# Block sums of Strassen-type weights: formed on VectorE, or added into SBUF by accumulating transfers

## Chip, cores and metric

The kernel runs on 1 core of one Trainium2 chip. The metric is device time in microseconds (us), the median of several runs. 1964.19 us is the median of 3 runs of the kernel before, which lie between 1963.92 and 1965.04 us.

## What is computed

The reference is a two-layer transformer on 512 tokens of width 1024. Each layer has a feed-forward network (FFN), a mixer, and a second FFN; there are four FFNs in all. The change is in the FFNs.

```python
def swiglu(h, w_in, w_out):
    a, b = jnp.split(h @ w_in, 2, axis=-1)
    return (jax.nn.silu(a) * b) @ w_out

for layer in range(DEPTH):
    g = norm_g[layer]
    x = x + 0.5 * swiglu(rmsnorm(x, g[0]), ffn_w_in[layer, 0], ffn_w_out[layer, 0])
    h = rmsnorm(x, g[1])
    ...
    x = x + 0.5 * swiglu(rmsnorm(x, g[2]), ffn_w_in[layer, 1], ffn_w_out[layer, 1])
```

`w_in` is 1024 x 5632, `w_out` 2816 x 1024, all float32.

## The kernel before

**Precision.** Every matrix is split into a high part (float32r, a rounded copy made on ScalarE, ACT) and a low part (the difference, made on VectorE, DVE). One product of two matrices is then three matmuls: high by high, high by low, low by high.

**Seven products.** `h @ w_in` is done with a scheme that needs seven products of half-size blocks in place of eight. The 22 tiles of each half of `w_in` go in 11 pairs. Each pair p has four weight blocks of 128 x 1024 floats (512 KB): a11, a21, a12 and a22. Its products take these left sides: p1 a11, p2 a12, p4 a22, and the sums p5 a21 + a22, p6 a21 + a22 - a11, p3 a12 - (a21 + a22 - a11), p7 a11 - a21. `Products.side` (lines 131 to 151) makes each sum with one VectorE instruction over 128 x 1024: L142, L145, L148, L150. `Products.make` (L153) then makes the split: `whi` on ScalarE (L159) and `wlo` on VectorE (L160), into a pool `wsp` with three slots of each. The right sides (sums of halves of x) are made once per FFN by `combined` (L215), tile by tile, into `th` and `tl`.

**Order of the work.** PE follows the program's order exactly. `round_` (L402) goes through a list of products; ahead of each it asks for the splits of the next three. One product is 24 matmuls (L332). `ORDER` (L105) is p1, p5, p2, p6, p3, p7, and p4 comes one pair later, behind the next pair's p1. In each FFN the pairs go in three rounds (0 to 4, 5 to 8, 9 and 10); behind each round stands a part of the product with `w_out` ("down", lines 383 to 397), which needs the results of the pairs so far. On the other engines a scheduler sets the order when the program is built.

**Loads.** All blocks come from DRAM on SP's queue (`fetch`, L121). `wraw` has two buffers, each with a pair's a11 and a21; a22 has two buffers and a12 one. A load waits till the split that last read its buffer is done.

**Norm.** The row scale is summed from `ss` (L255 on POOL), by four small matmuls (`rstd_cols`, L280, asked for at pair 0's p6), Ln and Exp on ScalarE (L267, L268), four small DVE steps (the last writes `Rc`, L272) and four transposes on PE (`rstd_rows`, L294, asked for at pair 0's p3).

**ScalarE's tables.** Ln, Exp and Silu need a function table. `lnexp` (L175) loads one that holds both Ln and Exp ahead of a stage that wants them; where a function's table isn't loaded, the build puts a load (ACT_TABLE_LOAD) ahead of the instruction.

Of the kernel before, what the change touches and what calls it, by code (L numbers as in the profile page):

```python
# [8 lines left out]
F32 = mybir.dt.float32  # L9
# [3 lines left out]
OP = mybir.AluOpType  # L13
# [28 lines left out]
class Filler:  # L42
# [5 lines left out]
    def add(self, name, gen):  # L48
        self.q.append((name, gen))
# [49 lines left out]
class Products:  # L99
# [2 lines left out]

    ORDER = ("p1", "p5", "p2", "p6", "p3", "p7", "p4")  # L105

    def __init__(self, b, src):
        self.b, self.src, self.parts, self.blocks = b, src, {}, {}
# [1 line left out]
    def place(self, p, early):  # L110
# [7 lines left out]
        else:  # L118
            w["a12"] = b.wx.tile([128, 1024], F32, name="a12", bufs=1)

    def fetch(self, p, n):  # L121
        c = ("a11", "a21", "a12", "a22").index(n) * 1024
        self.b.nc.sync.dma_start(self.blocks[p][n], self.src[p, :, c:c + 1024])

    def load(self, p, early):
        if p < NP and ("a11" if early else "a12") not in self.blocks.get(p, ()):
            self.place(p, early)
            for n in ("a11", "a21", "a22") if early else ("a12",):
                self.fetch(p, n)

    def side(self, p, q):

        w, v = self.blocks[p], self.b.nc.vector
        if q == "p1":
            return w["a11"]
        if q == "p2":
            return w["a12"]
        if q == "p4":
            return w["a22"]
        if q == "p5":  # L140
            w["s"] = self.b.wx.tile([128, 1024], F32, name="ws", bufs=1)
            v.tensor_add(w["s"], w["a21"], w["a22"])  # L142
            return w["s"]
        if q == "p6":
            v.tensor_sub(w["s"], w["s"], w["a11"])  # L145
            return w["s"]
        if q == "p3":
            v.tensor_sub(w["a12"], w["a12"], w["s"])  # L148
            return w["a12"]
        v.tensor_sub(w["a21"], w["a11"], w["a21"])  # L150
        return w["a21"]

    def make(self, p, q):  # L153
        if (p, q) in self.parts:
            return
        b = self.b
        x = self.side(p, q)
        o = b.wtile(1024)
        b.nc.scalar.activation(o[0], x, AF.Copy)  # L159
        b.nc.vector.tensor_sub(o[1], x, o[0].bitcast(F32))  # L160
        self.parts[p, q] = o


class Builder:
# [50 lines left out]
    def combined(self, i, gcol):  # L215

        nc, v = self.nc, self.nc.vector
        j, x = i // 2, self.X[:, i].rearrange("p (h t) -> p h t", h=2)

        def parts(n, m, src):  # L220
            h, l = self.TH[j][:, n:n + m], self.TL[j][:, n:n + m]
            nc.scalar.activation(h, src, AF.Copy)  # L222
            v.tensor_sub(l, src, h.bitcast(F32))  # L223

        if i % 2 == 0:

            e = self.E = self.xp.tile([128, 3, HT], F32, name="te")
            nc.scalar.activation(e[:, 0:3:2], x, AF.Copy, scale=gcol)
            v.tensor_sub(e[:, 1], e[:, 2], e[:, 0])
            parts(B11, 2, e[:, 0:2])  # L230
        else:

            e, o = self.E, self.xp.tile([128, 5, HT], F32, name="to")
            nc.scalar.activation(o[:, 0:2], x, AF.Copy, scale=gcol)
            parts(B21, 2, o[:, 0:2])
            v.tensor_sub(o[:, 2], o[:, 1], e[:, 1])
            v.tensor_sub(o[:, 3], o[:, 0], o[:, 2])
            v.tensor_sub(o[:, 4], o[:, 1], e[:, 2])
            parts(T2, 3, o[:, 2:5])

# [71 lines left out]
    def ffn(self, n, after, first=None):  # L312
# [5 lines left out]
        nc = self.nc  # L318
# [15 lines left out]
        def copy(name, bank, bufs):  # L334
            t = self.ft.tile([128, 2, HT], F32, name=name, bufs=bufs)
            nc.scalar.activation(t, bank.rearrange("p (f t) -> p f t", f=2), AF.Copy)
            return t

        def run(p, q, R):

            v = nc.vector
            three = lambda b: b.rearrange("p (f t) -> p f t", f=2)
            if q == "p1":
                d = st[p] = {"a": self.bank("ps")}
                product(p, q, d["a"], B11, True)
                d["c1"] = copy("c1", d["a"], 1)
                return
            d = st[p]
            if q == "p5":
                d["b"] = self.bank("pt")  # L350
                product(p, q, d["b"], T1, True)
                d["c5"] = copy("c5", d["b"], 1)
            elif q == "p2":
                c = self.bank("s")
                product(p, q, c, B21, True)
                d["t"] = self.ft.tile([128, 2, 2, HT], F32, name="ta", bufs=2)
                v.tensor_add(d["t"][:, :, 0], d["c1"], three(c))
            elif q == "p6":
                product(p, q, d["a"], T2, False)
                d["c2"] = copy("c2", d["a"], 1)  # L360
            elif q == "p3":
                product(p, q, d["b"], B22, False)
                v.tensor_add(d["t"][:, :, 1], d["c2"], three(d["b"]))
                t = d["t"].rearrange("p f h t -> p f (h t)")
                v.tensor_mul(t, t, R()[:, None, :].to_broadcast([128, 2, S]))
                self.table = "silu"
                nc.scalar.activation(t, t, AF.Silu)
            elif q == "p7":
                product(p, q, d["a"], T3, False)
                v.tensor_add(d["c5"], d["c5"], three(d["a"]))  # L370
            else:
                product(p, q, d["a"], T4, False)
                t = d["t"]
                v.tensor_mul(t[:, :, 1], t[:, :, 1], d["c5"])
                v.tensor_mul(t[:, :, 0], t[:, :, 0], three(d["a"]))
                h = [self.hp.tile([128, 2, S], F32R, name=x) for x in ("hh", "hl")]
                t = t.rearrange("p f h t -> p f (h t)")
                nc.scalar.activation(h[0], t, AF.Copy)
                v.tensor_sub(h[1], t, h[0].bitcast(F32))  # L379
                H[p] = h  # L380
                del st[p]
# [11 lines left out]

        def down_end(d, bank, R):
            t = self.ft.tile([128, S], F32, name="dn", bufs=1)
            nc.vector.scalar_tensor_tensor(t, bank, 0.5, R, op0=OP.mult, op1=OP.mult)  # L396
            nc.vector.tensor_add(self.X[:, d], self.X[:, d], t)

        tags = ("s", "s", "s", "pt", "o")
# [1 line left out]
        R = lambda: Rt[0]  # L401
# [19 lines left out]
        for g, (a, b) in enumerate(GROUPS):  # L421
            last = b == NP
            seq = []
            for p in range(a + 1 if g else a, min(b + 1, NP)):
                ps = [(p, q) for q in Products.ORDER[:6]]
                if p:
                    ps.insert(1, (p - 1, "p4"))
                seq += ps
            round_(a, seq + [(NP - 1, "p4")] * last)
            banks = {}  # L430

            def begin(d):
                w = down_w(g, d)
                w.split(0)
                banks[d] = w, self.bank(tags[d % 5])

            def sums(d, pairs):
                down_mm(g, d, *banks[d], pairs)

            def end(d):  # L440
                down_end(d, banks.pop(d)[1], R())
                if last:
                    after(d)

            begin(0)
            begin(1)
            if last:
                self.next_in()
                self.lnexp()
                sums(0, range(a, b - 1))  # L450
                run(NP - 1, "p4", R)
                sums(1, range(a, b - 1))
                for d in range(2):
                    sums(d, [b - 1])
                    end(d)
                begin(2)
            for d in range(2 if last else 0, KT):
                if d + 1 < KT and d + 1 not in banks:
                    begin(d + 1)
                sums(d, range(a, b))  # L460
                if d == KT - 2:
                    W.load(b + 1, True)
                end(d)
# [691 lines left out]
    def build(self):  # L1155
        from contextlib import ExitStack
        with ExitStack() as ctx:
            nc, tc = self.nc, self.tc
# [61 lines left out]
            first = None  # L1220
# [4 lines left out]
            if kind(0) == "ffn":  # L1225
                self.wx = tc.alloc_tile_pool(name="wx", bufs=1)
                first = Products(self, self.i["ffn_in"][int(st[0][3])])
                first.place(0, True)
                first.place(0, False)
                for i, n in ((0, 0), (1, "a11"), (2, 0), (3, "a21"), (4, 0), (5, "a22"), (6, 0), (7, "a12")):  # L1230
                    xdma(i)
                    if n:
                        first.fetch(0, n)
            else:
                for i in range(KT):
                    xdma(i)
# [116 lines left out]
```

## Time and profile before

| | |
|---|---|
| median of 3 runs | 1964.19 us |
| the profiled execution | 1967.51 us, its span 1965.6 us |
| PE busy | 1872.4 us, 95% |
| DVE busy | 1481.5 us, 75% |
| ACT busy | 908.5 us, 46% |
| POOL busy | 226.8 us, 12% |
| DMA | 198.16 MB, mean 101 GB/s |

Times are read from one profiled execution. "L332" is line 332 of the kernel. PE is TensorE's matmuls, PEld its weight loads, DVE VectorE, ACT ScalarE, POOL GpSimd, SP the engine that issues most transfers ("SPq" is an issue). An arrow `<-` behind an idle time names what ended it.

### The profile page before, as it was taken

What the parts mean: (1) busy time and instruction counts of PE and PEld (TensorE: products, weight loads), DVE (VectorE), ACT (ScalarE), POOL (GpSimd) and SP (SyncE); (2) the same over time, 40 slices, a digit from 0 to 9 for tenths busy, and PEclk for the clock granted to TensorE, in tenths of its full rate; (3) what the DMA queues carried; (4) which work ended last, traced back from release to release, by engine and by line L of the source; (5) the groups of instructions that cost most, each with busy time, mean ns of one, the idle gap of its engine ahead of it and who ended that gap; (6) DMA issues with size and microseconds to landing.
All of it is one profiled execution on the core that took longest, in us unless ns stands there. A gap on an engine that the chain in (4) does not pass through costs nothing.

```text
span 1965.6 us, 30669 instructions
## 1 busy us (share of the span) xinstructions
PE 1872.4 (95%) x12448; PEld 1682.0 (86%) x12448; DVE 1481.5 (75%) x1929; ACT 908.5 (46%) x1275; POOL 226.8 (12%) x218
## 2 busy tenths in 40 slices
PE   4999999999999899999979999999999989999997
PEld 3999989887877898999879899897776779989896
DVE  7977958657466895876889688675898688869684
ACT  5543525434354452443555345254537555435343
POOL 2000000200162000000010000002258320000001
PEclk9999999999899899999989999999999989999998
DMA  4333241313332224232313323224256132323412
GB/s 154 97 108 107 85 126 52 120 65 105 106 102 76 91 92 129 98 101 90 112 64 108 119 92 113 86 76 143 74 158 174 38 115 97 105 93 103 129 47 83
DMA packets 60509, 198.16 MB, mean 101 GB/s; under 512 B 7880, under 2 KB 8056, under 8 KB 57296
## 3 DMA queue, kind: packets, MB, share of 16 engines
q1 hardware_dynamic: 57712, 191.65, 30.8%
q10 hardware_dynamic: 2304, 4.20, 0.9%
q8 instruction: 97, 1.59, 0.3%
q0 software_dynamic: 352, 0.36, 0.1%
q14 instruction: 44, 0.36, 0.1%
HBM read 178.03 MB, written 2.15 MB: 92 GB/s over the span
## 4 chain that ended last, share of the span: by engine, by line
PE 82%; DVE 12%; ACT 2%; issue 2%; DMA 1%; SPq 0%; POOL 0%; DVEq 0%; ACTq 0%; POOLq 0%
PE ps L332 25%; PE pt L332 13%; PE s L332 6%; PE s L199 6%; PE s L200 6%; PE s L198 6%; PE ps L198 3%; PE ps L199 3%; PE ps L200 3%; DVE tl L223 2%; DVE acc L1108 1%; PE s L621 1%; PE pt L198 1%; PE pt L199 1%; PE pt L200 1%
## 5 line engine op out<-in xcount | busy, mean ns | idle before, releaser
L332 PE MATMUL ps<-th,whi 128*128 128x256 f32 x1408 | 395.5, 281 | 28.0 <-ACT th L222 15.2
L332 PE MATMUL ps<-tl,whi 128*128 128x256 f32 x1408 | 395.2, 281 | 7.8 <-DVE tl L223 7.8
L332 PE MATMUL ps<-th,wlo 128*128 128x256 f32 x1408 | 394.6, 280 | 1.0 <-DVE wlo L160 1.0
L84 ACT ACTIVATE whi<-wraw 128x1024 fp32r<-128x1024 f32 (+3 forms) x156 | 157.1, 1008 | 334.9 <-PE s L199 128.0
L332 PEld LDWEIGHTS ps<-th,whi 128*128 128x128 f32 x1408 | 266.4, 189 | 29.3 <-ACT th L222 15.9
L332 PEld LDWEIGHTS ps<-tl,whi 128*128 128x128 f32 x1408 | 266.4, 189 | 9.7 <-DVE tl L223 9.1
L332 PEld LDWEIGHTS ps<-th,wlo 128*128 128x128 f32 x1408 | 266.5, 189 | 1.3 <-DVE wlo L160 1.3
L159 ACT ACTIVATE whi<-a 128x1024 fp32r<-128x1024 f32 x132 | 140.2, 1062 | 154.1 <-PE pt L332 50.4
L332 PE MATMUL pt<-th,whi 128*128 128x256 f32 x704 | 200.9, 285 | 9.0 <-ACT whi L159 9.0
L199 PE MATMUL s<-hl,whi 128*128 128x512 f32 x528 | 206.0, 390 | 0.9 <-DVE hl L379 0.9
L198 PE MATMUL s<-hh,whi 128*128 128x512 f32 x528 | 205.6, 389 | 0.0
L200 PE MATMUL s<-hh,wlo 128*128 128x512 f32 x528 | 205.5, 389 | 0.0
L255 POOL TENSOR_TENSOR ss<-ss,sq 128x512 f32<-128x512 f32 x48 | 72.2, 1504 | 1154.5 <-ACT sq L251 827.6
L88 DVE TENSOR_TENSOR wlo<-wraw,whi 128x1024 fp32r<-128x1024 f32 (+3 forms) x144 | 170.7, 1185 | 43.3 <-ACT whi L84 42.3
L332 PE MATMUL pt<-th,wlo 128*128 128x256 f32 x704 | 200.6, 285 | 2.8 <-DVE wlo L160 2.8
L332 PE MATMUL pt<-tl,whi 128*128 128x256 f32 x704 | 200.3, 285 | 0.0
L160 DVE TENSOR_TENSOR wlo<-a,whi 128x1024 fp32r<-128x1024 f32 x132 | 160.9, 1219 | 7.9 <-ACT whi L159 7.9
L159 ACT ACTIVATE whi<-wraw 128x1024 fp32r<-128x1024 f32 x88 | 93.4, 1061 | 145.6 <-PE ps L332 55.8
L396 DVE SCALAR_TENSOR_TENSOR dn<-s,R 128x512 f32<-128x512 f32 x72 | 49.7, 690 | 131.4 <-PE s L200 131.3
L332 PEld LDWEIGHTS pt<-th,whi 128*128 128x128 f32 x704 | 136.5, 194 | 9.4 <-ACT whi L159 9.4
L332 PEld LDWEIGHTS pt<-th,wlo 128*128 128x128 f32 x704 | 136.6, 194 | 3.3 <-DVE wlo L160 3.3
L332 PEld LDWEIGHTS pt<-tl,whi 128*128 128x128 f32 x704 | 136.4, 194 | 0.0
(288 smaller groups left out, 4285.6 us busy)
## 6 DMA issues: line engine op xcount, KB each, us to landing
wraw<-in_ffn_in_dram SPq DMA_DIRECT2D x88, 512.0 KB, 4.8
a<-in_ffn_in_dram SPq DMA_DIRECT2D x88, 512.0 KB, 3.7
wraw<-in_ffn_out_dram SPq DMA_DIRECT2D x64, 512.0 KB, 3.5
wraw<-in_ffn_out_dram SPq DMA_DIRECT2D x32, 384.0 KB, 3.1
x<-x SPq DMA_DIRECT2D x62, 128.0 KB, 2.3
wraw<-in_even_fox_dram SPq DMA_DIRECT2D x4, 1024.0 KB, 5.0
wraw<-in_even_out_dram SPq DMA_DIRECT2D x4, 1024.0 KB, 5.6
wraw<-in_odd_q_dram SPq DMA_DIRECT2D x8, 512.0 KB, 3.2
```

What stands on the lines that cost most here:

```text
L84: nc.scalar.activation(hi, x, AF.Copy)
L88: nc.vector.tensor_sub(lo, x, hi.bitcast(F32))
L159: b.nc.scalar.activation(o[0], x, AF.Copy)
L160: b.nc.vector.tensor_sub(o[1], x, o[0].bitcast(F32))
L198: mm(ps, w[0], x[0], start=first, stop=False)
L199: mm(ps, w[0], x[1], start=False, stop=False)
L200: mm(ps, w[1], x[0], start=False, stop=last)
L223: v.tensor_sub(l, src, h.bitcast(F32))
L255: nc.gpsimd.tensor_tensor(self.ss, self.ss, sq, op=OP.add)
L332: mm(o, w[:, c], x, start=fresh and f == j == i == 0, stop=j == 3 and i == 2, skip_group_check=True)
L396: nc.vector.scalar_tensor_tensor(t, bank, 0.5, R, op0=OP.mult, op1=OP.mult)
L621: nc.tensor.matmul(s[:, :n], q[hh][:, b * 128:b * 128 + 128], k[hh][:, :n], start=k is kh, stop=k is kl)
```

## The change

The four sums per pair are no longer made on VectorE. A block is added to another where it lies, in SBUF, by a transfer from DRAM that accumulates (`add`, issued on POOL's queue). a21 is the running sum: a22 is added when a21 has been loaded (that is p5's left side), a11 when p5's split has read it (p6), a12 when p6's split has read that (p3). a11 gets a21 when p1's split has read it (p7). The signs of b's sums and of the last step are turned round (L229, L236, L237, L396) so that all sums of blocks are plain additions. The products' order becomes p1, p5, p6, p2, p7, p3, with p4 of the pair before behind p5. The first loads come in another order, and `c5` has two buffers.

```diff
-    ORDER = ("p1", "p5", "p2", "p6", "p3", "p7", "p4")
+    ORDER = ("p1", "p5", "p6", "p2", "p7", "p3", "p4")
+    BLOCKS = ("a11", "a21", "a12", "a22")
+    SIDE = dict(p1="a11", p2="a12", p3="a21", p4="a22", p5="a21", p6="a21", p7="a11")
+    THEN = dict(p1=("a11", "a21"), p5=("a21", "a11"), p6=("a21", "a12"))
...
+    def add(self, p, n, m):
+
+        self.b.nc.gpsimd.dma_start(self.blocks[p][n], self.block(p, m), accum_op=OP.add)
...
-            for n in ("a11", "a21", "a22") if early else ("a12",):
+            for n in ("a21", "a11", "a22") if early else ("a12",):
                 self.fetch(p, n)
+            if early:
+                self.add(p, "a21", "a22")
...
     def make(self, p, q):
...
-        x = self.side(p, q)
+        x = self.blocks[p][self.SIDE[q]]
         o = b.wtile(1024)
         b.nc.scalar.activation(o[0], x, AF.Copy)
         b.nc.vector.tensor_sub(o[1], x, o[0].bitcast(F32))
         self.parts[p, q] = o
+        if q in self.THEN:
+            self.add(p, *self.THEN[q])
...
-            v.tensor_sub(o[:, 2], o[:, 1], e[:, 1])
-            v.tensor_sub(o[:, 3], o[:, 0], o[:, 2])
+            for k, x in ((1, e[:, 1]), (0, o[:, 2])):
+                v.scalar_tensor_tensor(o[:, 3 - k], x, -1.0, o[:, k], op0=OP.mult, op1=OP.subtract)
...
-                d["c5"] = copy("c5", d["b"], 1)
+                d["c5"] = copy("c5", d["b"], 2)
...
-            nc.vector.scalar_tensor_tensor(t, bank, 0.5, R, op0=OP.mult, op1=OP.mult)
+            nc.vector.scalar_tensor_tensor(t, bank, -0.5, R, op0=OP.mult, op1=OP.mult)
...
-                    ps.insert(1, (p - 1, "p4"))
+                    ps.insert(2, (p - 1, "p4"))
...
-                for i, n in ((0, 0), (1, "a11"), (2, 0), (3, "a21"), (4, 0), (5, "a22"), (6, 0), (7, "a12")):
+                for i, n in ((0, "a21"), (1, "a11"), (2, 0), (3, "a12"), (4, 0), (5, 0), (6, "a22"), (7, 0)):
...
+                first.add(0, "a21", "a22")
```

**POOL, pairs 1 to 3 of the first FFN.** Before, POOL has no transfer there. Now it has four per pair. `wraw_252` is the buffer of pair 1, `wraw_468` of pair 2, `wraw_696` of pair 3, `wraw_924` of pair 4:

```order
L135 DMA wraw_252<-in_ffn_in_dram 128x1024
L135 DMA wraw_468<-in_ffn_in_dram 128x1024
L135 DMA wraw_252<-in_ffn_in_dram 128x1024 x2
L135 DMA wraw_468<-in_ffn_in_dram 128x1024
L135 DMA wraw_696<-in_ffn_in_dram 128x1024
L135 DMA wraw_468<-in_ffn_in_dram 128x1024 x2
L135 DMA wraw_696<-in_ffn_in_dram 128x1024
L135 DMA wraw_924<-in_ffn_in_dram 128x1024
L135 DMA wraw_696<-in_ffn_in_dram 128x1024 x2
```

Between the add behind a pair's p1 (its first row here) and the add behind its p5 (the first of its "x2", the second is p6's) stands the first add of the next pair. The same order comes at pairs 6 and 7, and in each FFN; at the other pairs the two adds follow each other.

**ScalarE, the start of the first FFN, as it is now.** `wraw_105` is pair 0's a11 (first row here with it), then a21; `th1`, `th2` and `th3` hold tiles of x that p1 needs:

```order
L151 ACTIVATE whi_206<-wraw_105 128x1024
...
L245 ACTIVATE sq_145<-X_78 128x512
L151 ACTIVATE whi_211<-wraw_105 128x1024
L216 ACTIVATE th1_95<-te_140 128x512
...
L151 ACTIVATE whi_216<-wraw_105 128x1024
L216 ACTIVATE th2_96<-to_168 128x768
L216 ACTIVATE th3_97<-te_180 128x512
```

The splits of p5 and p6, which need an added block, stand ahead of tiles that p1 needs.

**ScalarE, the start of the first mixer.** Before:

```order
L267 ACTIVATE rs_y<-Ra 128x4
L268 ACTIVATE rs_y<-rs_y 128x4
L84 ACTIVATE whi<-wraw 128x1024 x2
L300 ACTIVATE R<-pt 128x512
```

and now:

```order
L261 ACT_TABLE_LOAD
L261 ACTIVATE rs_y<-Ra 128x4
L262 ACT_TABLE_LOAD
L262 ACTIVATE rs_y<-rs_y 128x4
L84 ACTIVATE whi<-wraw 128x1024 x2
L294 ACTIVATE R<-pt 128x512
```

The scheduler now puts `lnexp`'s load ahead of an FFN's last Silu, which loads another table over it. The build then loads one table for each Ln and another for each Exp. The program has 47 table loads where it had 9: four that bring Silu's table back, 22 in the first mixer, 4 in the second, 2 at the norm of each FFN but the first, and 2 at the final norm.

## Rows read from the trace of the kernel before

**Rows 1.** Page, part 1: busy time, share of the span, instructions.

```profile
PE 1872.4 (95%) x12448; PEld 1682.0 (86%) x12448; DVE 1481.5 (75%) x1929; ACT 908.5 (46%) x1275; POOL 226.8 (12%) x218
```

**Rows 2.** Windows: us, then PE, PEld, DVE, ACT, POOL busy, PEclk, DMA share, GB/s.

```profile
46.00:128.00 82.00, 82.00 (x705) 82.00 (x704) 71.70 (x71) 45.87 (x51) 0.00 (x0) 1.00 0.29 92
380.00:638.00 258.00, 251.72 (x1485) 206.74 (x1485) 155.92 (x269) 114.17 (x215) 57.60 (x75) 0.97 0.29 90
```

**Rows 3.** Chain in time: start us, us, work; three products, then one.

```profile
88.27 8.40 PE ps L332 x72
96.67 2.80 PE pt L332 x24
```

**Rows 4.** Groups by line, VectorE: busy us, mean ns | idle before.

```profile
L150 DVE TENSOR_TENSOR wraw<-wraw 128x1024 f32<-128x1024 f32 x44 | 54.7, 1244 | 0.3
...
L142 DVE TENSOR_TENSOR ws<-wraw,a 128x1024 f32<-128x1024 f32 x44 | 53.6, 1218 | 0.1
```

**Rows 5.** Timeline, one pair: start us, us, engine line; SP issues.

```profile
96.64 1.06 ACT L159 ACTIVATE whi<-ws 128x1024 fp32r<-128x1024 f32 x1 [1.25 <-PE ps L332]
...
98.17 1.22 DVE L160 TENSOR_TENSOR wlo<-ws,whi 128x1024 fp32r<-128x1024 f32 x1
...
86.23 0.80 SPq L123 DMA_DIRECT2D wraw<-in_ffn_in_dram  x2
91.49 11.80 SPq L123 DMA_DIRECT2D a<-in_ffn_in_dram  x2
```

**Rows 6.** DMA queues and issues: KB each, median us from issue to landing.

```profile
q1 hardware_dynamic: 57712, 191.65, 30.8%
...
wraw<-in_ffn_in_dram SPq DMA_DIRECT2D x88, 512.0 KB, 4.8
...
wraw<-in_ffn_out_dram SPq DMA_DIRECT2D x64, 512.0 KB, 3.5
...
wraw<-in_even_vg_dram SPq DMA_DIRECT2D x2, 1024.0 KB, 4.9
...
p<-in_t_onehot_dram POOLq DMA_DIRECT2D x2, 40.0 KB, 2.6
```

**Rows 7.** Waits of PE, whole run: us in total, times, longest.

```profile
PE ps L332 <- ACT th L222: 15.2, 3, 7.5
...
PE s L294 <- DVE Rc L272: 11.4, 4, 3.0
PE pt L332 <- ACT whi L159: 9.0, 2, 4.5
...
PE pt L332 <- DVE wlo L160: 2.8, 2, 1.5
```

**Rows 8.** Timeline at the starts of the first and the second FFN.

```profile
8.11 1.48 DVE L237 TENSOR_TENSOR to<-to 128x256 f32<-128x256 f32 x1
...
17.87 0.41 DVE L237 TENSOR_TENSOR to<-to 128x256 f32<-128x256 f32 x1
...
22.69 2.29 DVE L150 TENSOR_TENSOR wraw<-wraw 128x1024 f32<-128x1024 f32 x1
...
616.47 8.20 SPq L123 DMA_DIRECT2D wraw<-in_ffn_in_dram  x4
...
641.79 1.21 DVE L142 TENSOR_TENSOR ws<-wraw,a 128x1024 f32<-128x1024 f32 x1
...
644.15 0.39 PE L332 MATMUL pt<-th,whi 128*128 128x256 f32 x1 [4.49 <-ACT whi L159]
...
660.96 0.65 PE L294 MATMUL s<-ident,Rc 128*128 128x128 f32 x4 [2.95 <-DVE Rc L272]
```

**Rows 9.** Chain in time at the start of the second FFN: 22, 23, 24 matmuls.

```profile
646.20 5.06 PE pt L332 x22
...
655.09 2.81 PE ps L332 x23
661.61 4.36 PE pt L332 x24
```

**Rows 10.** Windows there; columns as in rows 2.

```profile
646.20:651.20 5.00, 5.00 (x23) 5.00 (x24) 4.93 (x5) 1.06 (x1) 0.00 (x0) 0.50 0.00 0
655.00:657.90 2.90, 2.90 (x25) 2.80 (x25) 2.46 (x4) 0.35 (x1) 0.00 (x0) 1.00 0.68 209
661.90:665.90 4.00, 4.00 (x23) 4.00 (x22) 0.00 (x0) 0.36 (x2) 0.00 (x0) 0.57 0.02 4
```

**Rows 11.** Table loads by line; Ln after its wait in the last stage.

```profile
L179 ACT ACT_TABLE_LOAD x5 | 6.4, 1283 | 0.8 <-PEq L1342 0.7
...
1954.57 0.21 ACT L267 ACTIVATE rs_y<-Ra 128x4 f32<-128x4 f32 x1 [1.73 <-DVE Ra L285]
```

More of the change, by code (lines that the diff above doesn't have):

```diff
@@ L119, in place, with block @@
             w["a12"] = b.wx.tile([128, 1024], F32, name="a12", bufs=1)
+    def block(self, p, n):
+        c = self.BLOCKS.index(n) * 1024
+        return self.src[p, :, c:c + 1024]
     def fetch(self, p, n):
-        c = ("a11", "a21", "a12", "a22").index(n) * 1024
-        self.b.nc.sync.dma_start(self.blocks[p][n], self.src[p, :, c:c + 1024])
+        self.b.nc.sync.dma_start(self.blocks[p][n], self.block(p, n))
+    def add(self, p, n, m):
+        self.b.nc.gpsimd.dma_start(self.blocks[p][n], self.block(p, m), accum_op=OP.add)
     def load(self, p, early):
@@ L127, in load @@
             self.place(p, early)
-            for n in ("a11", "a21", "a22") if early else ("a12",):
+            for n in ("a21", "a11", "a22") if early else ("a12",):
                 self.fetch(p, n)
[L131 to L151, printed above, removed]
+            if early:
+                self.add(p, "a21", "a22")
     def make(self, p, q):
@@ L228, in combined @@
             nc.scalar.activation(e[:, 0:3:2], x, AF.Copy, scale=gcol)
-            v.tensor_sub(e[:, 1], e[:, 2], e[:, 0])
+            v.tensor_sub(e[:, 1], e[:, 0], e[:, 2])
             parts(B11, 2, e[:, 0:2])
```

## Prediction

> **What bounds the kernel now.** The page's busy shares come first: PE is busy for 95% of the span, DVE for 75% [rows 1]. A mean says nothing about one stage, so the next view is the windows. Over four pairs of the first FFN, 46 to 128 us, PE is busy for 82.00 of 82.00 us at a granted clock of 1.00, with DVE at 71.70 us and the DMA engines at 0.29 [rows 2]. The chain in time shows the same: three products take 8.40 us and one takes 2.80 us, all of it on PE [rows 3]. So DVE's sums, though they cost 54.7 to 53.6 us on each of four lines [rows 4], lie wholly beside PE there. **Taking them away buys nothing between pairs.** What can be bought lies where PE waits: in the FFN products that is 9.0 + 2.8 us for a split ("pt", which is p5's), 11.4 us for the norm's `Rc` and 15.2 us for tiles of x [rows 7], all at the starts of FFNs.
>
> **What the change removes at the starts.**
> The norm: PE's transposes waited four times for `Rc`, 2.95 us in the second FFN [rows 8]. The chain there began when the product before p6 was done and had one product of 2.80 us to hide under, so it is 2.80 + 2.95 = 5.8 us long. The new order puts three products (p6, p2, p7) in that place, 8.4 us. The chain grows too: in three FFNs two table loads of 1.283 us [rows 11] stand in it, which makes 5.8 + 2.6 = 8.4 us, about even. I take 0.5 us left in each, so -11.4 + 2 = -9.4 us. Behind that wait the granted clock was 0.57, which is the lower level of 1.2 GHz for most of the stretch [rows 10], and the next product took 4.36 us [rows 9] in place of 2.80. I count this for two FFNs: -3.1 us. Together -12.5.
> p5's split: in the second and fourth FFN PE waited 4.49 us for it and then for `wlo` [rows 7, 8], because the sum on L142 stood in DVE's queue at 641.79 us behind tiles of x [rows 8]. Now a22 is added by a transfer. The blocks are asked for at 616.47 us [rows 8]; 4.8 us for a load [rows 6] and some 5 us for the add (below) end by 627, ahead of need. That is -11.8 us. Behind the wait 22 matmuls took 5.06 us at a clock of 0.50 [rows 9, 10], 5.5 us for 24 against 2.80: -2.7 us twice. I take back 1.4 us in each, since p6's order now asks earlier for the row sums that POOL makes. Together -14.4.
> Third FFN: DVE's two sums stood among the tiles of x: -2 us.
> The new signs change one DVE form for another of the same shape: 0, hidden under PE, or the same if exposed.
>
> **What the change adds on ScalarE.** 38 table loads of 1.283 us, 49 us in all [rows 11]. The final norm's two are bare, since ScalarE has nothing to do between Ln and Exp and PE waits behind them: the Ln starts at once on `Ra` [rows 11]; one of the two fits in its 1.73 us of idle time, so 1.3 to 2.6 us. In the first mixer (380 to 638 us) ScalarE is busy for 114.17 of 258 us and PE for 251.72 [rows 2]: PE waits for 6 us in all, so the chains through ScalarE have slack there. The 22 loads there cost between 0 and 28 us. I take 7, a quarter, nearer the low end since PE so seldom waits; with the second mixer's 4 and the final norm, +10. The rest lie under PE.
>
> **The first start.** p5's split stands in ScalarE's order ahead of tiles that p1 needs, and now waits for a21 and then for an add; p6's split stands likewise. On the other side two DVE sums (one took 2.29 us while POOL worked [rows 8]) leave p1's path. Bounds -3.5 and +6; I take +3.
>
> **Sum without the adds' own delay: -12.5 - 14.4 - 2 + 3 + 10 = -16 us.**
>
> **The price of an accumulating transfer.** No row shows one. A plain 512 KB block moves in P: a 1024 KB load lands 4.9 - 3.5 = 1.4 us later than one of 512 KB [rows 6], and 30.8% of 1965.6 us for 191.65 MB [rows 6] makes 1.7 us for a block. So P is 1.4 to 1.7 us. An accumulating transfer has two streams to read, the block from DRAM and the old sum from SBUF. Its time T is at least P, if the second stream goes beside the first, and at most about 3P = 5.1 us, if all three streams go in turn. The nearest row is the 1024 KB load, which is two streams through the same 16 DMA engines: 2P = 2.8 to 3.4; as PE's loads leave these engines idle for 0.71 of the time, I take a little under it, **T = 2.6 us**. The fixed part is some 2.4 us, from the 2.6 us that POOL's 40 KB took to land [rows 6]. So an add alone lands 5.0 us after its issue.
> The Trainium skill says in "Collectives: The Full Stack", section "The bandwidth ceiling", that an add in the DMA engines runs at half the rate of a copy because it needs two source reads, not because the addition itself costs time. By that rule T would be 2P, 2.8 us or more, and no run here shows it yet; at 2.8 the sum below would be some 12 us higher.
>
> **What the adds delay.** Take t = 0 at the end of the product that frees a `wsp` slot for p5's split. ScalarE starts such a split at once (96.64 against 96.67 us [rows 3, 5]); 1.06 us for `whi` and 1.22 for `wlo` [rows 5] end it at 2.3. p1's split ended one product earlier, at -0.5. On POOL's queue stand p1's add, in five pairs per FFN (1, 2, 3, 6, 7) the next pair's first add, and then p5's add, which p6's split waits for. They move one behind another, beside a plain load or so (SP has two loads in line in that stretch [rows 5]). p5's add lands at -0.5 + 2.4 + 3T + P = 1.9 + 7.8 + 1.4 = 11.1. p6 starts four products after t = 0, at 11.2, and its split needs 2.3, so 8.9 is wanted: **2.2 us late, in 20 pairs, +44 us**. The other pairs have two adds in line and land at 8.5: no cost. The next link, p6's add for p3, has 8.4 us more of products for 5.0 + 2.3, so it holds. Behind p6's split on ScalarE stand p2's, `c5`'s copy and p7's, all shifted together, within this.
>
> **Forecast.** -16 + 44 = +28 us. The profiled execution (1967.51) stood 3.3 us above the median (1964.19); from the median the forecast is **1992 us**. Its own range, for T from 2.4 to 3.0 us, is 12 us lower to 24 us higher, and up to 40 more if such waits lower the clock as in rows 10: 1980 to 2055.
>
> **Rivals.**
> *The adds fit* (ends on the other side: faster). If T is at most 1.7 us, p5's add lands at 1.9 + 5.1 + 1.7 = 8.7, in time, and only the -16 us remains: 1948 us, or 1943 to 1962 with the table loads' bounds. It decides at T near 2.1, where 20 small waits pay for the starts. For it: DMA engines at 0.29 in these stretches. Against it: two streams. Chance 0.28.
> *The DMA engines become the bound.* At T = 4.0, p5's add lands at 15.3, 6.4 us late; 20 x 6.4 = 128, and 12 pairs with two adds in line are 2.4 late, 29. A wait that long also lowers the clock, 2.6 us for each of the 20: +52. With -16 that is +193: 2157 us. Four adds and four loads per pair are then 4 x 4.0 + 4 x 1.5 = 22 us of engine time for 19.6 us of products, so nothing catches up. For it: three streams in turn are possible. Chance 0.20.
> *POOL is held while it issues.* A POOL instruction and DVE instructions with two inputs slowed each other: the same form on L237 took 1.48 us beside POOL and 0.41 alone [rows 8]. If an issue on POOL loses as much, 1.1 us, two of the three in line cost 2.2 us more per pair: 1992 + 20 x 2.2 = 2036. In "SBUF — State Buffer", section "Who interferes with whom", the Trainium skill says that DVE with two inputs contends with a POOL instruction that reads SBUF, not with one that only writes; by that rule this rival is unlikely, and the rows can't say: what slowed DVE in them was an addition on POOL, which does read SBUF. Chance 0.12.
>
> **How the numbers follow.** The forecast has 0.40, the rivals 0.28, 0.20 and 0.12. About 0.2% (4 us) can be told from no change. Faster by that: 0.25 of the first rival and 0.02 of the forecast's low end, 0.27. Within it: 0.06. Slower: 0.67. The range takes in the first rival whole and most of the second: 1943 to 2130, since a T above 3.6 or so is left outside.
>
> **What would show it.** The issues "wraw<-in_ffn_in_dram POOLq" x176, with their time to landing: under 5 us at the median speaks for the first rival, 5 to 9 for the forecast, more for the second. In the windows PE should be below its full share between pairs, with waits of "ps" for ACT `whi` at p6 about 20 times. The waits for `Rc` and "pt" should be gone, the table loads 47. Were PE still busy for all of a stretch of pairs, the price of the adds is wrong; were the wait at p3 and not at p6, the link named is.

## The result, and the profile after

The changed kernel took **2140.82 us**, the median of 4 runs from 2136.87 to 2146.04 us; the kernel before, run beside it, 1964.08 us. The ratio is 1.0900, 95% interval 1.0876 to 1.0925: slower, and outside the predicted range of 1943 to 2130 us. The profiled execution took 2141.77 us, its span is 2140.0 us, 174.4 us longer than before.

Page, part 1, of the changed kernel (answers to [rows 1]):

```profile
PE 1932.2 (90%) x12448; PEld 1725.6 (81%) x12448; DVE 1283.7 (60%) x1753; ACT 947.9 (44%) x1313; POOL 374.7 (18%) x394
```

VectorE is 197.8 us lighter without its sums. PE, which runs the same 12448 matmuls, is busy for 59.8 us more, and its idle time rose from 1965.6 - 1872.4 = 93.2 to 207.8 us, by 114.6 us. The two make up the 174.4.

Windows of the changed kernel: the same 82 us of the first FFN as in [rows 2], and two parts of one pair that is looked at below (columns as there: us, PE, PEld, DVE, ACT and POOL busy, PEclk, DMA share, GB/s):

```profile
46.00:128.00 82.00, 71.85 (x576) 70.42 (x575) 47.12 (x48) 36.66 (x42) 11.93 (x14) 0.96 0.70 165
...
88.60:94.20 5.60, 5.58 (x46) 5.44 (x46) 4.06 (x4) 2.15 (x3) 0.85 (x1) 1.00 0.68 117
96.90:99.90 3.00, 3.00 (x14) 3.00 (x15) 2.46 (x3) 0.90 (x1) 0.25 (x1) 0.50 0.41 104
```

In the stretch where PE had no idle time before, it now has 10 of 82 us, and ran 576 matmuls where it ran 705. The DMA engines went from 0.29 to 0.70.

Waits of PE, whole run: us in total, times, longest (answer to [rows 7]):

```profile
PE ps L326 <- ACT c L330: 74.1, 41, 3.1
PE ps L326 <- ACT whi L151: 34.1, 16, 10.8
PE ps L326 <- ACT th L216: 18.7, 4, 7.0
PE o L274 <- POOL ss L249: 14.9, 2, 7.8
PE ps L326 <- DVE wlo L152: 14.6, 20, 1.2
...
PE ps L288 <- DVE Rc L266: 3.5, 1, 3.5
```

The waits for `Rc` of 11.4 us and of "pt" for p5's split are gone, as predicted. But the largest wait is one that the prediction does not have: 41 times for `c` on L330, the copy of the bank `ps` behind p6 (the variable `c2`). Only 16 waits are for a split `whi`. The longest of those, 10.8 us, is PE's first wait of all, at the start of the program; the kernel before has it too, with 12.8 us.

The timeline of one pair shows it. POOL first (start us, us, engine, line, what; in brackets the idle time before and what ended it), then ScalarE, then PE:

```profile
74.67 0.85 POOL L135 DMA_DIRECT2D wraw<-in_ffn_in_dram  x1 [9.85 <-DVE wlo L152]
76.97 0.86 POOL L135 DMA_DIRECT2D wraw<-in_ffn_in_dram  x1 [1.46 <-DMA wraw<-in_ffn_in_dram]
79.03 0.85 POOL L135 DMA_DIRECT2D wraw<-in_ffn_in_dram  x1 [1.21 <-DVE wlo L152]
88.86 0.85 POOL L135 DMA_DIRECT2D wraw<-in_ffn_in_dram  x1 [8.98 <-DVE wlo L152]
```

```profile
86.24 1.06 ACT L151 ACTIVATE whi<-wraw 128x1024 fp32r<-128x1024 f32 x1 [3.34 <-DMA wraw<-in_ffn_in_dram]
...
95.31 1.06 ACT L151 ACTIVATE whi<-wraw 128x1024 fp32r<-128x1024 f32 x1 [3.86 <-DMA wraw<-in_ffn_in_dram]
96.27 0.58 ACT L330 ACTIVATE c<-ps 128x512 f32<-128x512 f32 x1
```

```profile
88.62 0.39 PE L326 MATMUL ps<-th,wlo 128*128 128x256 f32 x1 [0.64 <-DVE wlo L152]
...
96.90 0.58 PE L326 MATMUL ps<-th,whi 128*128 128x256 f32 x1 [2.64 <-ACT c L330]
```

POOL issues p1's add at 74.67, the next pair's first add at 76.97, p5's add at 79.03 and p6's at 88.86. p5's add lets p6's split go at 86.24, p6's add lets p3's split go at 95.31, 6.45 us after its issue. In ScalarE's order, as the scheduler set it, p3's split stands ahead of `c2`'s copy. The copy could have run when p6 had left the bank, at about 91.4; it ran at 96.27. And PE needs it early: p7 goes into the same bank, and between p6 and p7 stands only p2. So p7 waited 2.64 us, not for its own weights but for a copy that stood behind another product's split. Behind the wait the granted clock was 0.50, which is 1.2 GHz, for 3 us (third window above).

DMA queues and issues (answer to [rows 6]): packets, MB, share of 16 engines; KB each, median us from issue to landing.

```profile
q1 hardware_dynamic: 57712, 191.65, 27.8%
q0 software_dynamic: 25696, 92.65, 24.8%
...
wraw<-in_ffn_in_dram POOLq DMA_DIRECT2D x176, 512.0 KB, 6.2
wraw<-in_ffn_in_dram SPq DMA_DIRECT2D x88, 512.0 KB, 4.7
a<-in_ffn_in_dram SPq DMA_DIRECT2D x88, 512.0 KB, 6.2
```

An add's time T in the engines: 24.8% of 2140.0 us over 176 adds, 3.0 us, with what little else q0 carries and with its packets' waiting for others. A packet of 4 KB of an add takes 328 ns where one of a plain load takes 159 (medians of the packet records), 2.06 times as much; 8 packets on each engine make 2.6 us. The Trainium skill says of collectives in "Collectives: The Full Stack", section "The bandwidth ceiling", that an add needs two reads and so runs at half the rate of a copy. The 2.06 agrees with the half rate; that the two reads are the reason, no run here shows.

### The profile page after: what moved, and what is told of

Its sections match the earlier page's. It is cut to its first block, busy times and chain, and to the rows that moved or that the text cites. A ratio compares the mean times of both kernels' runs of the same rounds, so it can differ in the third digit from the quotient of the medians.

```text
span 2140.0 us, 30952 instructions
## 1 busy us (share of the span) xinstructions
PE 1932.2 (90%) x12448; PEld 1725.6 (81%) x12448; DVE 1283.7 (60%) x1753; ACT 947.9 (44%) x1313; POOL 374.7 (18%) x394
## 3 DMA queue, kind: packets, MB, share of 16 engines
q0 software_dynamic: 25696, 92.65, 24.8%
## 5 line engine op out<-in xcount | busy, mean ns | idle before, releaser
L326 PE MATMUL ps<-th,whi 128*128 128x256 f32 x1408 | 421.3, 299 | 127.0 <-ACT c L330 74.1
L152 DVE TENSOR_TENSOR wlo<-wraw,whi 128x1024 fp32r<-128x1024 f32 x220 | 269.2, 1223 | 345.5 <-ACT whi L151 337.4
L151 ACT ACTIVATE whi<-wraw 128x1024 fp32r<-128x1024 f32 x220 | 232.5, 1057 | 492.2 <-DMA wraw<-in_ffn_in_dram 305.0
L326 PE MATMUL ps<-th,wlo 128*128 128x256 f32 x1408 | 415.6, 295 | 14.7 <-DVE wlo L152 14.6
L326 PE MATMUL ps<-tl,whi 128*128 128x256 f32 x1408 | 414.3, 294 | 7.5 <-DVE tl L217 7.5
L326 PEld LDWEIGHTS ps<-th,whi 128*128 128x128 f32 x1408 | 285.1, 202 | 140.3 <-ACT c L330 82.5
L135 POOL DMA_DIRECT2D wraw<-in_ffn_in_dram x176 | 151.5, 891 | 1222.8 <-DVE wlo L152 741.2
L326 PEld LDWEIGHTS ps<-th,wlo 128*128 128x128 f32 x1408 | 286.0, 203 | 19.4 <-DVE wlo L152 19.4
L84 ACT ACTIVATE whi<-wraw 128x1024 fp32r<-128x1024 f32 (+3 forms) x156 | 157.0, 1007 | 320.5 <-PE s L193 114.6
L326 PEld LDWEIGHTS ps<-tl,whi 128*128 128x128 f32 x1408 | 285.8, 203 | 9.7 <-DVE tl L217 9.1
L151 ACT ACTIVATE whi<-a 128x1024 fp32r<-128x1024 f32 x88 | 92.7, 1053 | 95.9 <-PE pt L326 57.0
```

The source lines that it names most:

```text
L84: nc.scalar.activation(hi, x, AF.Copy)
L135: self.b.nc.gpsimd.dma_start(self.blocks[p][n], self.block(p, m), accum_op=OP.add)
L326: mm(o, w[:, c], x, start=fresh and f == j == i == 0, stop=j == 3 and i == 2, skip_group_check=True)
```

## The experiments

Three theories were tried. **Queue order:** p6's late add blocks p7 through ScalarE's order. **Transfers** (later also "engine time"): the DMA engines are simply full. After e1_pin a third came in, **late p5's add**: the predicted link, in POOL's queue; with the first it makes "two late adds". All ratios are to the kernel before, run beside each.

### e1_pin: p3's split behind `c2`'s copy

```diff
-        b.nc.scalar.activation(o[0], x, AF.Copy)
+        hi = b.nc.scalar.activation(o[0], x, AF.Copy)
+        if q == "p3":
+            b.tc.keep_in_program_order(hi)
```

> One line: on ScalarE the split of p3 is kept behind c2's copy, as the program has them. No sum, transfer or product changes. Theory 'queue order': p6's add lands 6.2 us after its issue, too late for p3's split; that split waits on ScalarE ahead of c2's copy, and the p7 products on PE wait for the copy (74.1 us in 41 waits, with the lower clock behind them). Then these waits fall below 10 us, what is left of the delay shows as smaller waits at p3 or p6, and the time is 1990 to 2040 us. Theory 'transfers': the DMA engines (busy for 0.70 of the time in these pairs) and the queue of adds set the pace, so the same time comes back at p3: 2110 to 2145 us.

Measured: 2125.54 us, ratio 1.0800 (1.0774 to 1.0825). The waits for `c` left the list, but their time came back in another place. Waits of PE, and of the same kernel the issues on POOL, the split on ScalarE and the wait on PE in a pair:

```profile
PE ps L328 <- ACT whi L151: 77.6, 23, 10.5
```

```profile
77.17 1.74 POOL L135 DMA_DIRECT2D wraw<-in_ffn_in_dram  x2 [1.48 <-DMA wraw<-in_ffn_in_dram]
...
88.28 1.06 ACT L151 ACTIVATE whi<-wraw 128x1024 fp32r<-128x1024 f32 x1 [8.55 <-DMA wraw<-in_ffn_in_dram]
...
89.39 0.58 PE L328 MATMUL ps<-th,whi 128*128 128x256 f32 x1 [5.28 <-ACT whi L151]
```

The two issues at 77.17 are the next pair's first add and p5's. The first of them had to wait for the block that it adds to, so it held POOL for 1.48 us with p5's add behind it. p5's add, third in line, let p6's split go at 88.28 only, and PE waited 5.28 us at p6. That is the predicted link, at the predicted place: without the 10.5 us at the program's start 22 waits where 20 were forecast, but 3.0 us each and not 2.2. The theory of the queue order alone fell by its numbers (1990 to 2040). The time lies in the range of "transfers" (2110 to 2145), but the wait came back at p6 and not at p3, where that theory had it; e8_both decides below. What the first theory missed: the waits for `c` had held PE back, so that p5's add came nearly in time.

### e2_plain: the same transfers without the addition

```diff
-        self.b.nc.gpsimd.dma_start(self.blocks[p][n], self.block(p, m), accum_op=OP.add)
+        self.b.nc.gpsimd.dma_start(self.blocks[p][n], self.block(p, m))
```

> The four transfers per pair on POOL's queue copy in place of accumulating, so the sums are left out (each block is overwritten by the one that should be added). The same bytes come from DRAM, in the same order with the same waits. A 4 KB packet should take about 159 ns in place of 328. Theory 'queue order': an add's time in the DMA engines falls by 1.3 us and its landing from 6.2 to about 4.9 us, in two links per pair, and the waits for c2's copy shrink but stay: 2030 to 2090 us. Theory 'transfers': engine time per pair falls by 5 us, the DMA share from 0.70 to some 0.45, nothing has to wait any more: 1945 to 1975 us. If the fixed part of a transfer is all that matters: over 2120 us.

Measured: 1982.02 us, ratio 1.0071 (1.0048 to 1.0095). DMA queue and issues, the group of the issues on POOL (busy us, mean ns | idle before), and PE's waits for `c` and for the row sums:

```profile
q0 software_dynamic: 25696, 92.65, 14.9%
...
wraw<-in_ffn_in_dram POOLq DMA_DIRECT2D x176, 512.0 KB, 4.5
```

```profile
L135 POOL DMA_DIRECT2D wraw<-in_ffn_in_dram x176 | 94.0, 535 | 1110.1 <-DVE wlo L152 673.5 <-DVE X L391 331.7 <-DMA wraw<-in_ffn_in_dram 83.6
```

```profile
PE o L274 <- POOL ss L249: 11.7, 2, 6.7
...
PE ps L326 <- ACT c L330: 5.9, 10, 1.5
```

With the same dependences, orders and bytes from DRAM, 159 of the 177 us are gone. A transfer takes 14.9% of 1978.6 us over 176, 1.7 us, in place of 3.0; it lands after 4.5 us in place of 6.2. So most of the loss hangs on what the addition costs. Both theories missed: the time is 7 us above what "transfers" expected and 48 us under what "queue order" did. Less traffic, an earlier landing and a shorter issue on POOL (535 ns) change together here, so this run can't tell them apart; the next ones do in part.

### e3_no_p7add: three adds per pair, p7's sum left out

```diff
-    THEN = dict(p1=("a11", "a21"), p5=("a21", "a11"), p6=("a21", "a12"))
+    THEN = dict(p5=("a21", "a11"), p6=("a21", "a12"))
```

> The add for p7 is left out (p7 multiplies a11 alone), so three adds per pair in place of four. Theory 'queue order': the late add is p6's, which has no other add ahead of it in most pairs; only p5's add moves up in the queue: 2090 to 2135 us, and the waits for c2's copy stay near 74 us. Theory 'transfers': a quarter of the adds' time in the DMA engines and on the queue is gone and with it well over a quarter of the delay: 2000 to 2080 us.

Measured: 2120.68 us, ratio 1.0772 (1.0753 to 1.0790). The wait for `c` stays:

```profile
PE ps L326 <- ACT c L330: 78.5, 34, 4.7
```

A quarter of the adds' traffic bought 20 us, where "transfers" expected 60 and more: engines that are simply full don't explain the loss.

### e9_first and e8_both: the next pair's first add behind p5's add

```diff
-            if early:
-                self.add(p, "a21", "a22")
+            if early and p - 1 in self.last:
+                with self.b.tc.issue_after(self.last[p - 1].ins):
+                    self.add(p, "a21", "a22")
+            elif early:
+                self.add(p, "a21", "a22")
```

(`self.last` holds p5's add of each pair.) The first alone, then with e1_pin's edit:

> The second repair alone: the next pair's first add behind p5's add on POOL's queue, ScalarE's order as in the change. Theory 'two late adds': the wait for c2's copy behind p3's split stays (74 us in 41 waits, and the clock with it), so 2080 to 2135 us. If p5's add was the cause and the other only followed from it: 1970 to 2050 us. Theory 'engine time': as the change, 2120 to 2145 us.

> Two repairs together: p3's split stays behind c2's copy on ScalarE (as in e1_pin), and on POOL's queue the next pair's first add goes behind p5's add, not ahead of it. With the first alone, 2125.5 us, the pairs that have the next pair's first add between p1's and p5's (indices 2, 3, 6 and 7 of each FFN) took 24 to 28 us and the others about 20. Theory 'two late adds': p6's add blocks p7 through ScalarE's order, and p5's add is late in POOL's queue; each alone is enough, so that mending one shows the other. Then both go: pairs near 20 us, 1970 to 2030 us. Theory 'engine time': the adds and loads of a pair fill the DMA engines, whatever the order: 2090 to 2125 us.

Measured: e9_first 2094.76 us, ratio 1.0658 (1.0639 to 1.0678); e8_both 2042.53 us, ratio 1.0386 (1.0370 to 1.0401). Waits of PE in e9_first, then in e8_both:

```profile
PE ps L331 <- ACT c L335: 78.7, 33, 4.9
...
PE ps L331 <- ACT whi L154: 10.5, 1, 10.5
```

```profile
PE ps L333 <- ACT whi L154: 23.3, 14, 10.7
PE ps L333 <- ACT th L223: 16.4, 4, 5.2
PE ps L333 <- DVE wlo L157: 15.5, 21, 1.2
PE o L281 <- POOL ss L256: 15.4, 2, 7.9
```

e9_first shows the one late add bare, in the range that "two late adds" gave for it, and e1_pin the other. Against 2140.82 us the edits give 15 and 46 us alone and 98 together: **two late adds, one behind the other**, of which each covers part of the other. 98 us of the loss is order, on ScalarE and in POOL's queue, with the same transfers. e8_both came out 12 us above the 1970 to 2030 that was expected, and 48 us under the 2090 that "engine time" expected at least; its pairs still take up to 24.5 us.

### e10_both_no_p7add: what is left in e8_both

The edits of e8_both and e3_no_p7add together.

> e8_both (2042.5 us) with the add for p7 left out (p7 multiplies a11 alone). In e8_both p5's add and p6's add still land 6 to 7 us after their issue, and 74 us are left over e5_order. Theory 'sharing': what is left comes from transfers that share the 16 DMA engines (busy for 0.76 of the time in the pairs) and the queue; with a quarter of the adds gone over half of it goes: 1975 to 2005 us. Theory 'serial': it is the time that each add of p5, p6 needs by itself, in a chain; p7's add has no part in it: 2025 to 2042 us.

Measured: 2005.36 us, ratio 1.0197 (1.0180 to 1.0214). Of the 74 us by which e8_both stands over e5_order, 37 went. That is just above the range of "sharing" (1975 to 2005, over half of the 74) and 20 us under that of "serial": about half goes with the fourth add, by its share of the engines and of the queue, and half stays with three. How the second half divides was not tried; 15.5 us of it is a wait for `ss` at two starts (below), which e10 still has.

### e4_tables and e11_both_tables: the extra table loads

```diff
-            self.tc.keep_in_program_order(self.nc.scalar.preload_act_table_set("natural_log_exp_and_others"))
+            load = lambda: self.nc.scalar.preload_act_table_set("natural_log_exp_and_others")
+            if self.last_silu is None:
+                self.tc.keep_in_program_order(load())
+            else:
+                with self.tc.issue_after(self.last_silu.ins):
+                    load()
```

e4_tables is the change with this edit, e11_both_tables is e8_both with it.

> The load of the table for Ln and Exp is kept behind the last Silu of an FFN on ScalarE, so the program has 9 table loads in place of 47. Nothing else changes by intent. Prediction: +10 us for the 38 loads, so 2126 to 2134 us now, all of it in the first mixer and the last norm. Rival: they are hidden under PE's work: 2138 to 2143 us.

> e8_both (2042.5 us) with the table load kept behind the last Silu. In e4_tables the first mixer became 15.3 us shorter and the FFNs 17 us longer, with the same order of work in them. If that was chance in the FFNs' waits for adds: 2022 to 2032 us here. If the extra table loads help the FFNs in some way: 2038 to 2046 us.

Measured: e4_tables 2142.47 us, ratio 1.0888 (1.0864 to 1.0912), no difference to the change; e11_both_tables 2029.37 us, ratio 1.0308 (1.0287 to 1.0329), 13.2 us less than e8_both. The 22 loads of the first mixer do cost time there: in the profile of e4_tables the stretch from the first FFN's last product to the second's first went from 306.1 to 290.8 us, while the four FFNs took 17.3 us more, with nothing changed in their order of work but the place of one split. Where each pair hangs on the landing of adds, the pairs' lengths scatter (the pair with index 1 took 24.8 to 30.3 us in the eight FFNs of these two profiles). That the 17.3 us are such scatter was not shown; e11_both_tables and h2_p5add_tables, where the gain comes through, speak for it.

### e5_order, h1_p5add and h2_p5add_tables: the change without the late adds

e5_order makes all four sums on VectorE, in place, with everything else as changed; h1_p5add (the edit shown) keeps only the first add of each pair; h2_p5add_tables is h1_p5add with the edit of e4_tables:

```diff
-    THEN = dict(p1=("a11", "a21"), p5=("a21", "a11"), p6=("a21", "a12"))
+    ON_V = dict(p6=("a21", "a21", "a11", OP.add), p7=("a11", "a21", "a22", OP.subtract), p3=("a21", "a21", "a12", OP.add))
...
+        if q in self.ON_V:
+            d, m, k, op = self.ON_V[q]
+            b.nc.vector.tensor_tensor(w[d], w[m], w[k], op=op)
```

> The new products' order, signs, buffers and first loads with no accumulating transfer at all: the four sums are made on VectorE, in place (p5's a21 + a22, p6's + a11, p7's as p6's sum - a22, p3's + a12). The prediction's parts without the adds: norm -12.5, p5's split -14.4 only if its sum leaves VectorE's queue (here it does not), third FFN 0, first start +3, table loads +10 to +15 (the first mixer was 15.3 us shorter without the extra loads): 1955 to 1970 us. If the order itself costs something (splits on ScalarE late): over 1975 us.

> Only the first sum, a21 + a22 for p5, is an accumulating transfer; it is issued when the blocks have been loaded and nothing stands behind it in POOL's queue. The other three sums are on VectorE as in e5_order. Theory 'two late adds': a single early add per pair is hidden, and at the starts of the second and fourth FFN p5's split is ready: e5_order less 5 to 15 us, 1945 to 1960 us. Theory 'engine time': one add per pair is a quarter of the adds, so 1975 to 2000 us.

> The version meant to beat both kernels: h1_p5add (only p5's sum by an accumulating transfer, the other three on VectorE; 1958.6 us) and the table load for Ln and Exp kept behind an FFN's last Silu (9 table loads in place of 47). If the 15.3 us that the first mixer lost to the extra loads come through: 1940 to 1948 us. If they are taken back elsewhere, as in e4_tables: 1954 to 1960 us.

Measured: e5_order 1968.75 us, ratio 1.0009 (0.9994 to 1.0025); h1_p5add 1958.62 us, ratio 0.9954 (0.9938 to 0.9970); **h2_p5add_tables 1938.06 us, ratio 0.9852 (0.9831 to 0.9873)**, which beats both kernels. Window of the same 82 us of e5_order, then page part 1, the same window, issues and waits of h2_p5add_tables:

```profile
46.00:128.00 82.00, 82.00 (x705) 82.00 (x705) 74.40 (x74) 45.95 (x51) 0.00 (x0) 1.00 0.34 104
```

```profile
PE 1860.8 (96%) x12448; PEld 1671.1 (86%) x12448; DVE 1434.4 (74%) x1885; ACT 906.9 (47%) x1275; POOL 266.1 (14%) x262
```

```profile
46.00:128.00 82.00, 82.00 (x705) 82.00 (x705) 70.97 (x70) 47.11 (x53) 2.55 (x3) 1.00 0.43 117
```

```profile
wraw<-in_ffn_in_dram POOLq DMA_DIRECT2D x44, 512.0 KB, 5.6
```

```profile
PE ps L333 <- ACT th L223: 24.7, 4, 9.3
PE ps L333 <- ACT whi L155: 10.7, 1, 10.7
PE ps L333 <- DVE tl L224: 6.4, 6, 1.7
...
PE ps L295 <- DVE Rc L273: 1.8, 1, 1.8
```

With VectorE at 70.97 of 82 us, PE is busy for 82.00 of 82.00 again, as in [rows 2]. So an add that lands 5.6 us after its issue costs PE nothing in these pairs, where it is the only one of its pair and its result is wanted long after. The ladder, in medians: order and signs alone 1968.75; the one early add takes 10.1 us off; three more adds, in the best order tried, put 83.9 on (2042.53); the order that the change had puts on 98.3 more. The table edit is worth 20.6 us in h2.

## Why the prediction was wrong, point by point

**What bounds the kernel: right.** PE was the bound between pairs, and VectorE's sums lay beside it: e5_order has all four of them, and in the 82 us of the first FFN PE is busy for 82.00 with 705 matmuls, as in the kernel before, with VectorE at 74.40.

**The starts: right in sum, less so term by term.** The sum of the norm, p5's split, the third FFN and the first start was -12.5 - 14.4 - 2 + 3 = -25.9 us. In h1_p5add, which has this part without the late adds, the spans from an FFN's first to its last product changed by +5.0, -12.2, -1.8 and -12.6 us and the first start by -2.0: -23.6 us. The second and fourth FFN came out as forecast, and of the waits for `Rc` in FFNs and for p5's split 0.7 us is left. But the third FFN gained less than its terms say. The first start and the first FFN are +3.0 together, with the norm's gain in them: PE waits 9 us longer there for tiles of x (24.3 over the whole run in place of 15.2), so the first start cost more than the +3 that was taken. That the sum is so near is in part luck. In e2_plain, which has all four transfers per pair but no additions, the four FFNs together took as long as before to within 1 us.

**But in the change itself part of that was given back.** I had taken back 1.4 us in each of two FFNs for the row sums. They cost 14.9 us in two waits, and 11.7 us in e2_plain. ScalarE at the second FFN's start, then POOL and PE:

```profile
699.26 1.06 ACT L151 ACTIVATE whi<-wraw 128x1024 fp32r<-128x1024 f32 x1 [9.83 <-DMA wraw<-in_ffn_in_dram]
700.23 0.71 ACT L228 ACTIVATE to<-X,gn 128x512 f32<-128x512 f32 x1
700.84 0.61 ACT L245 ACTIVATE sq<-X 128x512 f32<-128x512 f32 x1
```

```profile
701.61 1.43 POOL L249 TENSOR_TENSOR ss<-ss,sq 128x512 f32<-128x512 f32 x1 [10.80 <-ACT sq L245]
...
703.09 1.86 PE L274 MATMUL o<-ones,ss 128*128 128x1 f32 x8 [7.75 <-POOL ss L249]
```

p6's split waits 9.83 us for an add, and the last tile's square stands behind it on ScalarE; POOL's sum waits for the square, and PE for the sum. It is the same fault as at p7, a split that waits and holds what stands behind it. In h2_p5add_tables this wait doesn't occur.

**The table loads: +10 forecast, too low.** The first mixer, for which 7 us was taken, became 15.3 us shorter without them in e4_tables; over the whole program they measured 13.2 us on e8_both and 20.6 us on h1_p5add. In the change's whole time nothing can be told.

**T: right.** 2.6 us was taken; a packet's 328 ns make 2.6, and with the waiting for others it is 3.0, the end of the forecast's own range. The two streams that were argued for it give this size, and no run tells them from another reason. **The landing: mis-sized.** 2.4 us of fixed time was taken from POOL's 40 KB transfers, 5.0 us in all. The median landing is 6.2 us in the change, with waiting behind other transfers in it, and 5.6 us in h2_p5add_tables, where one add per pair is left.

**p5's add 2.2 us late in 20 pairs, +44 us: the mechanism right, the size too small.** In the change 15 such waits are left, 23.3 us (34.1 - 10.8), all in pairs that the prediction names; laid bare in e1_pin it is 22 waits, 67 us, of which 66.6 us lie at p6 of just the 20 pairs named, 3.3 us each, and the clock comes on top.

**The step that failed: "The next link, p6's add for p3, has 8.4 us more of products for 5.0 + 2.3, so it holds."** This link was put at nothing. I asked when p3 needs its split, and not what stands behind that split on ScalarE, which I did ask for p6's split. There stands `c2`'s copy, and p7 needs that one product earlier than p3 needs its split. In the pair shown p6 runs on from 88.62 and p7 could have started at 96.90 - 2.64 = 94.26, 5.6 us later. From the split's start to p7's passed 96.90 - 95.31 = 1.6 us, so the split had to start 4.0 us after 88.62; by p3's own need it had 8.4 - 2.3 = 6.1. The add was issued at 0.24 and took 6.45: 6.7, late by 2.6 for p7 and by only 0.6 for p3. With the 5.0 us that I had assumed it would have been in time for p3, but 1.2 late for p7. So the missing link alone would have cost something, and in this pair the mis-sized landing more than doubled it. It became the largest wait of the changed kernel, 74.1 us, half of the 149 us between the forecast of 1992 us and the result; behind 13 of the 19 that took 2 us or more a stretch at the lower clock follows. The prediction named a wait at p6, and as the sign of a wrong link one at p3; most of it was at neither, but at p7. Taking this link away alone (e1_pin) gives only 15 us back, since p5's add is then waited for in full: the two late adds have to be priced together, 98 us.

**The clock: seen, but kept out of the forecast.** "Up to 40 more" stood beside it. The mean granted clock of the profiled execution fell from 0.98 to 0.961. From these means and the spans, the time lost to the clock grew by some 44 us, an estimate: 0.039 x 2140.0 less 0.02 x 1965.6. PE's busy time rose by 59.8 us; what makes the rest is not shown.

**The rivals.** *The adds fit* failed in the change, since T is 3.0 us. Its own condition, T of 1.7 us, holds in e2_plain, and there almost nothing is waited for (5.9 us for `c`), but the time is 1982 and not 1948 us: even without late adds, the gain of some 26 us at the starts did not come there. The wait for the row sums is 11.7 us of that. *The DMA engines become the bound*: its 2157 us lies nearest to the result, but by another way: T is 3.0 and not 4.0 us, e3_no_p7add took away a quarter of the adds for 20 us, and 98 us went by order alone. Sharing of the engines is real but smaller, 37 us in e10. *POOL is held while it issues*: beside busy VectorE the 176 issues took a mean of 891 ns, those of the 44 adds in h2_p5add_tables 855 ns, so almost nothing of the 1.1 us.

## What to carry to other kernels

An instruction that waits for a transfer held up, here, everything behind it in its engine's order. So list what stands there, with the time at which each is wanted, and test the earliest of these deadlines, not that of the product itself. By these runs accumulating transfers pay only for sums that are wanted long after their inputs (here the first add of a pair, 44 of 176: faster by 0.5%, and by 1.5% with the table loads mended); the three others put 84 us on even in the best order tried. Where two waits lie on one chain, mending one shows the other: only mending both prices them.

## What had not been expected of the hardware

Issuing an accumulating transfer takes longer on POOL too: 0.85 us (mean 891 ns over the change) against 535 ns for the same transfer without the addition (e2_plain). And plain loads that share the engines land later: the loads of `a`, 3.7 us to land in the kernel before and in h2_p5add_tables, take 4.6 beside four plain transfers per pair in e2_plain and 6.2 beside four adds in the change.
